# A transformer layer's second feed-forward half step: hidden tiles by way of DRAM, and the output product as seven products of its blocks

## The chip, the cores and the metric

The kernel runs on one core of a Trainium2 chip. The metric is the device time of one execution, in microseconds. A profile is that of a single execution; its durations, and the sums made of them, belong to that execution's own span.

## The reference

One layer of a diffusion backbone over 1024 latent tokens of 1024 features, with 256 context tokens: a SwiGLU half step, token mixers (a short convolution and grouped-query attention side by side), a second SwiGLU half step, and a final RMSNorm. The change lies in the last two, which concern latent tokens alone:

```python
D_MODEL, SEQ, D_FF = 1024, 1024, 2816
def rms_norm(x, g):
    y = x * lax.rsqrt(jnp.mean(x * x, axis=-1, keepdims=True) + EPS)
    return y * g
def modulate(h, shift, scale):
    return h * (1.0 + scale) + shift
def swiglu(h, w_in, w_out):
    a, b = jnp.split(h @ w_in, 2, axis=-1)
    return (jax.nn.silu(a) * b) @ w_out
...
x = x + 0.5 * ml[8] * swiglu(modulate(rms_norm(x, norm3_g[layer]), ml[6], ml[7]),
                              ffn2_w_in[layer], ffn2_w_out[layer])
return rms_norm(x, final_g)
```

`ml[6..8]` are the shift, scale and gate that the layer derives from `c`, one value for each feature. Everything is float32.

## The kernel before, in words

**Layout and precision.** Activations lie with features in partitions: a tile is 128 features by 512 tokens. The 1024 latent tokens are two chunks, C0 and C1. A float32 operand of a product is split into two parts of the matmul's format fp32r, `hi` (a rounded copy) and `lo` (the rest): `split` (l. 186) is a cast on ACT (ScalarE) and a subtraction on DVE (VectorE). A product of two split operands takes three matmuls, hi·hi, hi·lo and lo·hi, all adding into one PSUM bank. "12 matmuls" below is four tiles of the contraction times three.

**Seven products instead of eight.** The class `Winograd` (l. 463) multiplies the weights of two column tiles a and b (blocks: halves of the 1024 input features) with the normalised latents (blocks: halves of the features by C0 and C1). A 2 x 2 block product needs eight products of blocks; Winograd's form needs seven, of sums and differences of the blocks. The seven right operands, from the latents, are made once in `norm0`, `norm1` (l. 499, 525) and stay in SBUF. The left operands are made for each pair of column tiles in `lefts` (l. 572): loads of the raw weights on SP's queue into tiles `raw` (3 buffers), sums `s1`, `s2`, `s3` on POOL (GpSimd), splits into tiles `wl` (4 buffers). `next_first`, `second` and `third` (l. 716 to 740) run the products 1 and 2, then 6, 7, 4, then 5, 3, 12 matmuls each, and add the outcomes from PSUM on DVE in tiles `u`, `v`, `c`, `b`.

**The second half step** is `Winograd.ffn` (l. 742), called at l. 1476 on the object `fast`, over 11 pairs of hidden tiles (2816 hidden features are 22 tiles of 128). For each hidden tile: the seven products of 12 matmuls give a and b of both chunks; `hidden` makes silu(a) * b and splits it into `hid` or `gh`, `gl`, in SBUF. After each pair comes its output product: for both chunks and each of 8 feature tiles, 2 hidden tiles x 3 = 6 matmuls with 512 columns into a fresh bank, 96 matmuls for the pair, and DVE adds the bank, times the gate, to x (one `scalar_tensor_tensor`). The weights for it, four blocks of `w_out`, come through `out_pieces` (l. 451), split into `wo`. With the last pair the second chunk goes in two parts of 256 tokens, and the final norm is run between.

**The final norm.** `final` (l. 1442) is a generator with two steps. The first squares x on ACT, sums the squares on DVE and POOL (`sum_squares`, l. 408), scales x by the gain into `yf` on ACT and derives 1/rms by token with tiny matmuls and a Newton step (`rstd_cols`, l. 240; `rs_a`, `rs_y`). The second turns `yf` back to tokens in partitions, groups of four 128 x 128 transposes into one PSUM bank, copied out times 1/rms by DVE and ACT in turn, and stores. It runs over three pieces: C0, and the two halves of C1. `after2` (l. 1469) says between which additions each step is traced.

**The first half step** already does what the second does not: `spill` (l. 963) stores silu(a) * b of a hidden tile in DRAM (`hd`), and a stage of its own (l. 1018 ff.) loads the hidden tiles back by chunk, splits them, and sums the output product over all 22 tiles in PSUM, without blocks.

**What sets the order.** A scheduler takes the instructions in the order in which they are traced as their priority and places them on each engine by its own estimate of when they can start; each engine then runs its list in that order. The SBUF comes from pools: `atile` (l. 111) takes one of 38 places of 4 KB a partition, `ttile` one of 11 of 2 KB. A tile that asks for a place waits for the last reader of the tile that had it. PSUM has eight banks: five with tag s (`ps_s`, l. 121), two with tag t and one with tag o. All engine calls go through a wrapper, so the profile puts every instruction at line 88; tiles are told apart by name, and names show as their stem (`ps`, `wl`, `raw`).

Of the kernel before, what the change touches and what calls it, by code (L numbers as in the profile page):

```python
# [49 lines left out]
def tile_dit_layer(  # L50
# [29 lines left out]
    class Engine:  # L80
        """An engine whose instructions stay in the order of the trace while strict[0] is set."""
# [72 lines left out]
    # Vectors over features become columns: one row of 128 each, transposed on the chip.  # L154
# [71 lines left out]
    def rsqrt_cols(a, n):  # L226
        """a ** -0.5 for a [P, n] > 0."""
# [12 lines left out]
    def rstd_cols(accs, n, dim):  # L240
        """(sum over accs and partitions + dim * eps) ** -0.5, tokens in partitions: [P, n / P]."""
# [12 lines left out]
    def bcast(y, n):  # L254
        """Columns y over tokens in partitions, as rows in all partitions: PSUM [P, n]."""
# [5 lines left out]
    def later_mod(m, halves=(0, 1), streams=None):  # L261
        """Columns of modulation m for the latents (0) and, where it is used, the context (1), in steps."""
# [54 lines left out]
    def first_mod(m, half, raws):  # L317
        """Half of modulation m of both streams, on the tensor engine alone; in steps: 6 tiles, 2, the columns."""
# [15 lines left out]
    def second_mod(m, half, raws):  # L334
        """The same of the latents alone; in steps: the products of each tile, their parts, their sums, the columns."""
# [23 lines left out]
    def norm_gain(name, m, gname):  # L359
        """g * (1 + scale) * sqrt(D) by stream; the shift is modulation m."""  # L360
# [59 lines left out]
    def modulated_norm(xs, hh, hl, ch, gain, mod, m):  # L420
        """In steps, for other work to be traced between: squares, sums, two halves of the rest."""
# [20 lines left out]
    def run(steps, n=None):  # L442
        """The next n steps (all without n)."""
# [7 lines left out]
    def out_pieces(w, js, spare=False):  # L451
        """Rows of w_out of hidden tiles js, by halves of the columns."""
# [10 lines left out]
    class Winograd:  # L463
        """Products with normalised latents by Winograd's seven products of 2 x 2 blocks.

        Blocks of the weights: two tiles of columns (a, b) by halves of the input features; blocks of
        the activations: halves of the features by halves of the tokens (C0, C1).
        """

        def __init__(self, xs, gain, mod, m, pairs, plain=False, ahead=3, side_from=None):  # L470
            """pairs: columns of each a and b; plain: with all parts of the latents themselves.

            ahead pairs are begun while the second tokens are normalised. side_from: from this pair on
            the plain left operands are given to side(i, operand) too, as 1, 2 (of a), 0, 4 (of b); those of
            the pairs before come after them.
            """
# [3 lines left out]
            self.n_ahead, self.side, self.started, self.n_left = ahead, None, [], 0  # L480
            self.source, self.ready = self.lefts(pairs, side_from), []

        def keep(self, i, k, src, lo_eng=None):
            """Feature tile k of right operand i."""
# [14 lines left out]
        def norm0(self, in_place=False):  # L499
            """In steps: squares, sums, two halves of the rest."""  # L500
# [13 lines left out]
        def square(self, d):  # L514
            """Feature tile d of the second tokens, squared, into the sums."""
            if d == 0:
                self.acc = [ttile("sq_acc")]
            sq = self.acc[0] if d == 0 else ttile("sq")
            act.activation(out=sq, in_=self.xs(d, C1), func=AF.Square)
            if d == KD - 1:  # L520
                self.acc.append(sq)
            elif d:
                dve.tensor_add(out=self.acc[0], in0=self.acc[0], in1=sq)

# [35 lines left out]
        def part_second(self, k):  # L560
            """The parts of tile k of the second tokens, in the place of the values."""
# [5 lines left out]
        def parts(self, k, ch):  # L567
            """Feature tile k of the latents, its two parts."""
# [3 lines left out]
        def lefts(self, pairs, side_from):  # L572
            """Left operands, in the order they are used."""
# [73 lines left out]
        def first(self):  # L647
            """The products with the first tokens alone: what the rest needs, and a of these tokens."""
# [5 lines left out]
        def start(self, norm):  # L654
            """The first products of some pairs, while the second tokens are normalised."""
# [17 lines left out]
        def start_together(self):  # L673
            """The same in steps: P1 of pairs 0, 1; of 2, 3; of each other; then the second products likewise."""
# [854 lines left out]
```

## Time and profile before

| | |
|---|---|
| time, median of 3 runs | 2813.86 us (2812.37 to 2816.64) |
| the profiled execution's span | 2813.7 us |
| granted TensorE clock | 0.9 or more in 37 of the 40 slices of the profile's row PEclk, 0.8 in the others |
| DMA | 298.77 MB, 106 GB/s on the mean |

How to read it: the page gives the busy time of each engine (PE is TensorE's matmuls, PEld its weight loads, SP issues most DMAs) as a share of the span, and the chain of work that ended last, with the share that each engine has in it. The costliest groups of instructions follow, each with its count, mean duration, and the idle time before it. The view by stretches gives the busy time of each engine in a window, with the number of instructions in brackets, then the granted clock, the DMA share and GB/s. A timeline lists instructions in order: the start in us, the busy time, the engine, what it does with the tile's name, its shape, how many of a kind in a row, and in square brackets how long the engine had been idle before and what it had waited for.

### The profile page before, as it was taken

Reading aid. Unit: us, or ns where it says so; the run is one execution under the profiler, and the core shown is the slowest. Engines: PE = TensorE matmul, PEld = TensorE weight load, DVE = VectorE, ACT = ScalarE, POOL = GpSimd, SP = SyncE. Lnnn points to the kernel's source line nnn. Section 1 sums busy time; section 2 is a strip of 40 time slices with the busy share of each in tenths; the row PEclk is TensorE's granted clock in tenths of the full one; section 3 lists DMA queues with packets and bytes.
Section 4 is the critical chain, followed back from the end, with each engine's and each line's share of the span. In section 5 each row is a group of like instructions: output and inputs, shape, how many; then the busy total and the mean of one; then the engine's idle time right before and its main releaser. Section 6 shows DMA issues by size and latency. Waiting matters only on the chain.

```text
span 2813.7 us, 37012 instructions
## 1 busy us (share of the span) xinstructions
PE 2725.5 (97%) x13741; PEld 2286.0 (81%) x13741; DVE 1957.2 (70%) x3218; ACT 1096.5 (39%) x2176; POOL 542.3 (19%) x433
## 2 busy tenths in 40 slices
PE   7898999999999989999999999999998999999998
PEld 4687988888888868888999888887886788888887
DVE  5886688877864387676568377776458766666667
ACT  3524333333433243333345167764245222232225
POOL 2541122121001054323123000000014221212111
PEclk8899999999999989999999999999999999999999
DMA  8264433445974333323313300002532311221111
GB/s 303 97 199 151 145 111 126 130 142 158 309 236 130 104 119 106 105 69 97 105 46 122 111 23 5 12 1 90 170 93 90 111 41 51 60 60 53 46 53 68
DMA packets 346910, 298.77 MB, mean 106 GB/s; under 512 B 25430, under 2 KB 276456, under 8 KB 346728
## 3 DMA queue, kind: packets, MB, share of 16 engines
q1 hardware_dynamic: 346728, 296.40, 32.9%
q8 instruction: 108, 1.77, 0.3%
q14 instruction: 74, 0.61, 0.1%
HBM read 247.54 MB, written 48.76 MB: 105 GB/s over the span
## 4 chain that ended last, share of the span: by engine, by line
PE 83%; DVE 9%; DMA 3%; issue 2%; ACT 2%; SPq 0%; POOL 0%; ACTq 0%; DVEq 0%; POOLq 0%
PE ps L88 73%; PE po L88 6%; PE pt L88 4%; DVE wl L88 2%; DVE r L88 1%; DVE nt L88 1%; DVE macc L88 1%; DMA raw<-in_ffn_w_out_dram 1%; DMA rawm<-in_w_mod_dram 1%; DVE wo L88 1%; DMA hid<-hd 1%; DVE h L88 1%; DVE uc L88 0%; SPq L88 0%; DMA mcol<-mrow 0%
## 5 line engine op out<-in xcount | busy, mean ns | idle before, releaser
L88 PE MATMUL ps<-r,wl 128*128 128x512 f32 x5280 | 1242.0, 394 | 36.9 <-ACT wl L88 12.8
L88 PEld LDWEIGHTS ps<-r,wl 128*128 128x128 f32 x5280 | 995.5, 190 | 256.1 <-ACT wl L88 16.4
L88 ACT CAST wl<-s 128x512 fp32r<-128x512 f32 x256 | 158.6, 620 | 330.3 <-PE ps L88 274.5
L88 ACT CAST wl<-raw 128x512 fp32r<-128x512 f32 x230 | 142.3, 620 | 245.7 <-PE ps L88 165.8
L88 DVE TENSOR_TENSOR wl<-raw,wl 128x512 fp32r<-128x512 f32 x228 | 167.1, 733 | 99.9 <-ACT wl L88 98.8
L88 DVE TENSOR_TENSOR wl<-s,wl 128x512 fp32r<-128x512 f32 x256 | 217.4, 850 | 11.6 <-ACT wl L88 9.8
L88 POOL TENSOR_TENSOR s<-raw,s 128x512 f32<-128x512 f32 x64 | 99.1, 1549 | 624.2 <-DVE wl L88 618.9
L88 PE MATMUL ps<-hid,wh 128*128 128x512 f32 x704 | 217.2, 390 | 1.4 <-ACT wh L88 1.4
L88 ACT CAST wh<-raw 128x1024 fp32r<-128x1024 f32 (+2 forms) x100 | 97.9, 982 | 251.5 <-PE ps L88 208.6
L88 DVE SCALAR_TENSOR_TENSOR x<-ps,gate_l,x 128x512 f32<-128x512 f32 (+1 forms) x200 | 140.7, 726 | 79.1 <-PE ps L88 78.8
L88 POOL TENSOR_TENSOR sq_acc<-sq_acc,sq 128x512 f32<-128x512 f32 (+1 forms) x33 | 41.8, 1268 | 765.4 <-ACT sq L88 764.6
L88 POOL TENSOR_TENSOR s<-raw 128x512 f32<-128x512 f32 x64 | 91.2, 1424 | 399.4 <-DMA raw<-in_ffn_w_in_dram 164.5
L88 DVE TENSOR_TENSOR wl<-raw,wh 128x1024 fp32r<-128x1024 f32 (+1 forms) x92 | 109.6, 1192 | 67.5 <-ACT wh L88 65.8
L88 PEld LDWEIGHTS ps<-hid,wh 128*128 128x128 f32 x704 | 131.7, 188 | 30.2 <-ACT wh L88 2.6
L88 DVE SCALAR_TENSOR_TENSOR macc<-rawm,silu_c,macc 128x512 f32<-128x512 f32 x168 | 141.4, 859 | 12.0 <-DMA rawm<-in_w_mod_dram 11.0
L88 PE MATMUL ps<-hid,wo 128*128 128x512 f32 (+1 forms) x552 | 147.7, 381 | 0.4 <-DVE x L88 0.3
L88 DVE TENSOR_TENSOR u<-u,ps 128x512 f32<-128x512 f32 x168 | 114.3, 680 | 46.6 <-PE ps L88 46.3
L88 PE MATMUL ps<-wh,r 128*128 128x256 f32 x768 | 141.5, 285 | 0.0
L88 PE MATMUL ps<-gh,wo 128*128 128x512 f32 (+1 forms) x368 | 135.5, 380 | 1.5 <-ACT wo L88 1.5
L88 PE MATMUL ps<-hid,wl 128*128 128x512 f32 x352 | 136.5, 389 | 0.0
L88 DVE TENSOR_REDUCE m<-ps 128x1 f32<-128x512 f32 (+1 forms) x192 | 112.7, 595 | 20.9 <-PE ps L88 19.8
L88 DVE TENSOR_TENSOR pts<-pt,pts 128x512 fp32r<-128x512 f32 x160 | 108.7, 683 | 18.8 <-ACT pts L88 18.4
(259 smaller groups left out, 4897.1 us busy)
## 6 DMA issues: line engine op xcount, KB each, us to landing
raw<-in_ffn_w_in_dram SPq DMA_DIRECT2D x114, 512.0 KB, 3.7
raw<-in_ffn_w_out_dram SPq DMA_DIRECT2D x76, 512.0 KB, 4.6
rawm<-in_w_mod_dram SPq DMA_DIRECT2D x128, 256.0 KB, 4.1
raw<-in_w_in_dram SPq DMA_DIRECT2D x57, 512.0 KB, 4.0
hid<-hd SPq DMA_DIRECT2D x44, 256.0 KB, 6.2
rawm<-in_w_mod_dram SPq DMA_DIRECT2D x16, 512.0 KB, 8.1
xd<-x SPq DMA_DIRECT2D x32, 256.0 KB, 8.6
x<-xd SPq DMA_DIRECT2D x32, 256.0 KB, 6.1
```

The source lines that it names most:

```text
L88: inst = getattr(self.engine, name)(*args, **kw)
```

## The change

`Winograd.ffn` is removed. The second half step first makes all 22 hidden tiles with `spill`, that is, silu(a) * b unsplit into DRAM; then `fetch_hidden` loads them back, 22 loads of 512 KB, each with both chunks of one hidden tile, into places of the large pool. Then `row_products` makes the output product as one stage, again by seven products of 2 x 2 blocks: the contraction is 22 hidden tiles in halves of 11 (`nk`), the output 8 feature tiles in halves of four, the tokens C0 and C1. Products are taken in the order 1, 2, 5, 6, 7, 4, 3. Each is 11 steps of 12 matmuls (4 feature tiles x 3) into four PSUM banks that stay for the whole product; an operand is split for each step into `wl` (left, from `ffn2_w_out`) and `wh` (right, from the hidden tiles), four buffers each. The sums for left operands (products 5, 6, 3 in tiles `ws`, 7 in the raw tile) and for right ones (5, 6, 7, 4, in place of the hidden tiles) are all `pool` operations. After each product the four banks go through additions on DVE in tiles `u` (`chain`), and each finished block is added to x by a `scalar_tensor_tensor` of 512 columns (`add3`): 24 of them, and 8 of 256 columns in product 3.

Product 3 (the first four features of C1) runs in two halves of 256 tokens; its 22 operands are split once into tiles of the large pool (`kept`) and used by both halves. `final` now begins with features 4 to 7, has an extra step between these and the rest, makes its scaled copies `yf` on DVE instead of ACT, and gives the squares of the last four features to the tiny matmuls one by one, without POOL. `after3` places it: the first two steps of C0 after product 4, its transposes after step 4 of the first half of product 3, the others further behind. `square` counts its calls in place of asking for feature 0. Comments and docstrings are dropped.

```diff
-        def ffn(self, w_o, gate, last_chunks, after):
...
+    def row_products(w, nk, raws, add, after=lambda i, k: None, halves=False):
...
+        def rows(t, k, lower, left, n=1):
+            o, c = k * P + R * lower, 512 * (not left)
+            load(t, w[o : o + n * P, c : c + 512].rearrange("(a p) n -> p a n", p=P))
...
+        def lefts(i):
+            for k in range(nk):
+                if i in (1, 2, 4, 3, 6):
+                    if k % 2 == 0:
+                        t, n = raw_tile(), min(2, nk - k)
+                        rows(t[:, :n], k, i in (2, 4, 3), i != 4, n)
+                    src = t[:, k % 2]
+                if i == 5:
+                    t = raw_tile()
+                    rows(t[:, :1], k, False, False)
+                    rows(t[:, 1:], k, True, False)
+                    if k % 2 == 0:
+                        sums[k] = atile("ws", (P, 2, 512))
+                    s = sums[k - k % 2][:, k % 2]
+                    pool.tensor_add(out=s, in0=t[:, 0], in1=t[:, 1])
+                    src = s
+                elif i in (6, 3):
+                    s = sums[k - k % 2][:, k % 2]
+                    if i == 6:
+                        pool.tensor_sub(out=s, in0=s, in1=src)
+                    else:
+                        pool.tensor_sub(out=s, in0=src, in1=s)
+                    src = s
+                elif i == 7:
+                    t = raw_tile()
+                    load(t[:], w[k * P : (k + 1) * P, :].rearrange("p (a n) -> p a n", a=2))
+                    pool.tensor_sub(out=t[:, 0], in0=t[:, 0], in1=t[:, 1])
+                    src = t[:, 0]
+                yield src
+        def right(i, k):
+            (b11, b12), (b21, b22) = ((t[:, 0], t[:, 1]) for t in (raws[k], raws[nk + k]))
+            if i == 5:
+                pool.tensor_sub(out=b11, in0=b12, in1=b11)
+            elif i == 6:
+                pool.tensor_sub(out=b11, in0=b22, in1=b11)
+            elif i == 7:
+                pool.tensor_sub(out=b12, in0=b22, in1=b12)
+            elif i == 4:
+                pool.tensor_sub(out=b11, in0=b11, in1=b21)
+            return {2: b21, 7: b12, 3: b22}.get(i, b11)
...
+        for i in (1, 2, 5, 6, 7, 4, 3):
+            if i == 3 and halves:
+                kept = []
+                for h in range(2):
+                    a, ps = h * 256, [ps_s(256) for _ in range(4)]
+                    for k, left in enumerate(lefts(i) if h == 0 else kept):
+                        if h == 0:
+                            kept.append((parts(left, None), parts(right(i, k), None)))
+                        l, r = kept[k]
+                        step(ps, k, l, r[:, :, a : a + 256])
+                        after(8 + h, k)
+                    for d in range(4):
+                        add(d, ("l", 512 + a, 256), ps[d])
+                    after(8 + h, nk)
+                break
+            ps = [ps_s() for _ in range(4)]
+            for k, left in enumerate(lefts(i)):
+                step(ps, k, parts(left, "wl"), parts(right(i, k), "wh"))
+                after(i, k)
+            for d in range(4):
+                if i == 1:
+                    chain[d] = ttile("u")
+                    act.copy(out=chain[d], in_=ps[d])
+                elif i == 2:
+                    c = ttile("c")
+                    dve.tensor_add(out=c, in0=chain[d], in1=ps[d])
+                    add(d, C0, c)
+                elif i == 5:
+                    add(d, C1, ps[d])
+                    add(d + 4, C1, ps[d])
+                elif i == 6:
+                    dve.tensor_add(out=chain[d], in0=chain[d], in1=ps[d])
+                    add(d, C1, chain[d])
+                elif i == 7:
+                    dve.tensor_add(out=chain[d], in0=chain[d], in1=ps[d])
+                    add(d + 4, C1, chain[d])
+                elif i == 4:
+                    dve.tensor_sub(out=chain[d], in0=chain[d], in1=ps[d])
+                    add(d + 4, C0, chain[d])
...
     def final(ch):
         s, o, n = ch
-        acc = sum_squares(xs, ch)
-        yk = []
-        for k in range(KD):
-            y = atile("yf")
-            act.activation(out=y[:, :n], in_=xs(k, ch), func=AF.Copy, scale=gf[:, k : k + 1])
-            yk.append(y)
-        rstd = rstd_cols([acc], n, D)
+        order = (4, 5, 6, 7, 0, 1, 2, 3)
+        acc, sqs, yk = ttile("sq_acc", n), [], {}
+        for k in order:
+            if k == 0:
+                yield
+            sq = ttile("sq", n) if k != 4 else acc
+            act.activation(out=sq, in_=xs(k, ch), func=AF.Square)
+            if k in (5, 6, 7):
+                dve.tensor_add(out=acc, in0=acc, in1=sq)
+            elif k < 4:
+                sqs.append(sq)
+            if k % 2 == 0:
+                y2 = atile("yf", (P, 2, 512))
+            yk[k] = y2[:, k % 2, :n]
+            dve.tensor_scalar(out=yk[k], in0=xs(k, ch), scalar1=gf[:, k : k + 1], scalar2=None, op0=ALU.mult)
+        rstd = rstd_cols([acc] + sqs, n, D)
         yield
...
+    fast.start(fast.norm1())
+    for j in range(NH):
+        u, c = fast.next_first()
+        v, b = fast.second(u)
+        spill(c, b, j, C0)
+        spill(*fast.third(u, v), j, C1)
+    hs = fetch_hidden()
...
+    def after3(i, k):
+        if (i, k) == (4, NH // 2):
+            run(finals[0], 2)
+        elif (i, k) == (8, 4):
+            run(finals[0])
+        elif (i, k) == (8, 7):
+            run(finals[1], 1)
+        elif (i, k) == (8, NH // 2):
+            run(finals[1], 1)
+            run(finals[2], 1)
+        elif (i, k) == (9, 5):
+            run(finals[1])
+    row_products(ffn2_w_out[0], NH // 2, hs, add3, after3, halves=True)
     run(finals[2])
```

More of the change, by code (lines that the diff above doesn't have):

```diff
@@ new lines, in row_products, with raw_tile, parts, step @@
+    def row_products(w, nk, raws, add, after=lambda i, k: None, halves=False):
+        R = P * nk
+        def rows(t, k, lower, left, n=1):
+            o, c = k * P + R * lower, 512 * (not left)
+            load(t, w[o : o + n * P, c : c + 512].rearrange("(a p) n -> p a n", p=P))
+        def raw_tile():
+            return wpool.tile([P, 2, 512], F32, tag="raw", name=uniq("raw"), bufs=3)
+        sums = {}
+        def lefts(i):
[38 more added lines that the diff above has]
+            return {2: b21, 7: b12, 3: b22}.get(i, b11)
+        def parts(src, tag):
+            if tag:
+                t = wpool.tile([P, 2, 512], F32R, tag=tag, name=uniq(tag), bufs=W_BUFS)
+            else:
+                t = atile("kept", (P, 2, 512), F32R)
+            split(src, t[:, 0], t[:, 1])
+            return t
+        def step(ps, k, l, r):
+            for d in range(4):
+                wh, wl = (l[:, v, d * P : (d + 1) * P] for v in range(2))
+                matmul(ps[d], wh, r[:, 0], start=k == 0, stop=False)
+                matmul(ps[d], wh, r[:, 1], start=False, stop=False)
+                matmul(ps[d], wl, r[:, 0], start=False, stop=k == nk - 1)
+        chain = {}
+        for i in (1, 2, 5, 6, 7, 4, 3):
[17 more added lines that the diff above has]
+                after(i, k)
+            for d in range(4):
+                if i == 1:
[17 more added lines that the diff above has]
+                    add(d + 4, C0, chain[d])
+                else:
+                    add(d, C1, ps[d])
+            after(i, nk)
```

67 lines of the change are left out of this document (16 added, 51 removed).

## The prediction

> **What bounds the kernel now.** First the page: its busy shares and the head of the chain that ended last.
>
> ```profile
> span 2813.7 us, 37012 instructions
> PE 2725.5 (97%) x13741; PEld 2286.0 (81%) x13741; DVE 1957.2 (70%) x3218; ACT 1096.5 (39%) x2176; POOL 542.3 (19%) x433
> PE 83%; DVE 9%; DMA 3%; issue 2%; ACT 2%; SPq 0%; POOL 0%; ACTq 0%; DVEq 0%; POOLq 0%
> ```
>
> TensorE is the bound. The median of the three runs is 2813.86 us, so next to nothing lies around the profiled span of 2813.7, and I add up against the span. Second, the busy times by stretch, for the half step that changes (columns: length, PE, PEld, DVE, ACT, POOL, granted clock, DMA share, GB/s).
>
> ```profile
> 2300.00:2760.00 460.00, 460.00 (x2031) 380.85 (x2030) 301.26 (x432) 127.51 (x216) 80.46 (x60) 1.00 0.17 51
> 2790.00:2813.70 23.70, 15.37 (x115) 13.99 (x114) 15.21 (x53) 14.33 (x32) 2.57 (x4) 0.87 0.44 179
> ```
>
> From 2300 to 2760 us PE never rests, while VectorE works 65% and GpSimd 17% of the time: there a matmul saved is time saved, as long as nothing else fills up. Third, the timelines: ACT's copies of u, one per hidden tile, and PE at the last output product.
>
> ```profile
> 2317.71 0.59 ACT L88 COPY u<-ps 128x512 f32<-128x512 f32 x1 [19.46 <-PE ps L88]
> 2377.55 0.59 ACT L88 COPY u<-ps 128x512 f32<-128x512 f32 x1 [20.95 <-PE ps L88]
> 2771.75 1.30 PE L88 MATMUL ps<-hid,wo 128*128 128x512 f32 x5
> 2799.11 0.28 PE L88 MATMUL ps<-gl,wo 128*128 128x256 f32 x1
> 2799.24 0.28 PE L88 MATMUL ps<-gh,wo 128*128 128x256 f32 x1
> ```
>
> Two hidden tiles with their output products take 59.84 us: 2 x 7 x 12 + 96 = 264 matmuls, so 0.2267 us for 512 columns. 256 columns start some 0.12 us apart. The last Winograd product ends at 2771.75.
>
> **1. PE work.** Removed: ten pairs x 96 x 0.2267 = 217.6 us, all of it before 2771.75, and the last pair (48 of 512 columns, 96 of 256), 22.4. Added: six products of 11 row tiles x 4 features x 3 = 132 matmuls each, 179.5 us, and the seventh in two halves, 264 x 0.12 = 31.7. Net 28.8 us less. The 192 additions to x out of PSUM go too, but DVE had room for them: nothing.
>
> The front of the half step keeps its order up to the first pair. The one wait of PE for an output weight there (1.5 us at 2199.8) goes; the denser pairs behind it may cost as much, since in the mixers' stage, equally dense, PE lost 2 us after its norm. I count zero (bounds -2 and +3), so the new stage begins at 2771.75 - 217.6 = 2554.1.
>
> **2. The hidden tiles come back from DRAM.** 22 loads of 512 KB. Two find free places early; the other 20 wait for the Winograd operands of the last hidden tile, the first of which come free 16 us before the stage begins, as they stand ahead of further weights in SP's queue. The nearest thing is the first half step, which reloads its hidden tiles in the same way:
>
> ```profile
> 740.00:750.00 10.00, 10.00 (x46) 8.03 (x45) 8.89 (x12) 8.20 (x13) 0.00 (x0) 1.00 1.05 389
> 770.72 0.73 PE L88 MATMUL ps<-hid,wh 128*128 128x512 f32 x2 [0.64 <-ACT wh L88]
> 772.22 0.73 PE L88 MATMUL ps<-hid,wh 128*128 128x512 f32 x2 [0.77 <-ACT wh L88]
> ```
>
> It moved up to 389 GB/s and cost PE 1.4 us. Here 11.5 MB, with the weights and the spills between, need about 31 us at 370 GB/s; they end 15 us into the stage, and the weights queued behind them are wanted at 16. I take 1.4 (bounds 0 and 6).
>
> **3. GpSimd and VectorE in products 5, 6, 7.** The change puts 88 sums of 128x512 on GpSimd: 11 left and 11 right operands each for products 5, 6 and 7, 11 rights for 4, 11 lefts for 3. Its order on the engine lets 20 to 24 of these run in products 1 and 2; 50 fall between the end of product 2 and that of 7. What one costs beside VectorE is seen where the norm fills both engines:
>
> ```profile
> 2154.76 1.72 POOL L88 TENSOR_TENSOR nt<-h,h 128x512 f32<-128x512 f32 x1
> 2156.43 1.73 POOL L88 TENSOR_TENSOR r<-nt,r 128x512 fp32r<-128x512 f32 x1
> 2158.13 1.72 POOL L88 TENSOR_TENSOR s<-raw,s 128x512 f32<-128x512 f32 x1
> 2175.08 1.29 POOL L88 TENSOR_TENSOR s<-s,raw 128x512 f32<-128x512 f32 x1
> 2176.33 1.73 POOL L88 TENSOR_TENSOR s<-raw,raw 128x512 f32<-128x512 f32 x1
> 2153.59 0.67 DVE L88 TENSOR_TENSOR uc<-uc,ps 128x512 f32<-128x512 f32 x1
> 2156.95 1.77 DVE L88 TENSOR_TENSOR r<-h,r 128x512 fp32r<-128x512 f32 x1
> 2158.64 1.76 DVE L88 TENSOR_TENSOR r<-nt,r 128x512 fp32r<-128x512 f32 x1
> 2162.01 0.68 DVE L88 TENSOR_TENSOR nt<-h,nt 128x512 f32<-128x512 f32 x1
> 2162.61 0.68 DVE L88 TENSOR_TENSOR r<-nt,r 128x512 fp32r<-128x512 f32 x1
> 2205.40 4.70 DVE L88 SCALAR_TENSOR_TENSOR x<-ps,gate_l,x 128x512 f32<-128x512 f32 x7 [3.06 <-PE ps L88]
> ```
>
> Alone, GpSimd starts a sum every 1.25 us and VectorE a subtraction every 0.60. Together each takes 1.69 for one of both: a GpSimd sum holds VectorE up by 1.09, unless that reads PSUM (the 0.67 row). Each step of a product (12 matmuls, 2.72 us of PE) needs two subtractions of two SBUF tiles, left and right. Over products 5 to 7 VectorE has 66 of them, 39.6 us; 8 additions to x from SBUF, 5.3; 16 operations out of PSUM, 10.1; and 42 sums that hold it up (8 of the 50 fit beside PSUM reads), 45.8: 100.8 us, where PE needs 3 x 29.9 = 89.7. **Loss 11 us.** Bounds: 0, if the four buffers of each operand take it up, and 22, if boundaries and the three raw buffers add as much again; 11 is the plain sum. In products 1, 2 and 4 the same sum stays below PE (50 of 55 us, 26 of 29.9).
>
> **4. The last product and the final norm.** Here the fixed order is against PE. In before, several banks turn the outputs, and the tail looks so:
>
> ```profile
> 1314.54 0.88 DVE L88 TENSOR_SCALAR y<-u,cols 128x512 f32<-128x512 f32 x2
> 2792.87 2.35 PE L88 MATMUL ps<-ident,yf 128*128 128x128 f32 x20
> 2794.66 1.27 ACT L88 ACTIVATE ot<-ps,rs_y 128x512 f32<-128x512 f32 x2 [0.43 <-DVE rs_y L88]
> 2799.56 0.48 DVE L88 SCALAR_TENSOR_TENSOR x<-ps,gate_l,x 128x256 f32<-128x256 f32 x1 [0.17 <-PE ps L88]
> 2800.45 1.02 ACT L88 ACTIVATE sq<-x 128x256 f32<-128x256 f32 x3
> 2803.52 0.60 PE L88 MATMUL pt<-ones,sq_acc 128*128 128x1 f32 x4
> 2804.16 0.16 DVE L88 TENSOR_SCALAR rs_a<-pt 128x2 f32<-128x2 f32 x1 [0.70 <-PE pt L88]
> 2806.12 0.16 DVE L88 SCALAR_TENSOR_TENSOR rs_y<-rs_t,rs_y 128x2 f32<-128x2 f32 x1
> 2807.30 1.26 ACT L88 ACTIVATE ot<-ps,rs_y 128x512 f32<-128x512 f32 x2 [1.50 <-PE ps L88]
> ```
>
> After the sixth product (call its end 0) VectorE first does 4 additions (the last ends at 2.0), 3 more of x and of squares (1.9), 8 scalings of 0.40 (3.2), and then the first pair of splits of product 3: PE waits until about 9. Until the scale of the first 512 tokens is known come 9 splits of 0.6, 2 sums of squares and 3 half ones, and the 2.2 us from rs_a to the last rs_y: 19.5. The four accumulators of a half leave one of the pool's five banks, and eight groups of transposes, ahead of the sixth step on PE, pass through it one by one: 0.65 to copy out, 0.5 to turn (4 of 0.118), some 0.3 for the two handovers, 1.45 x 7 + 0.65 = 11, so 30.5. Then 12 splits and 4 scalings, 8.4, and the last step: **the first half ends at 39**, where its matmuls alone are 15.8. The second half has its operands: 15.8, 16 transposes 1.9, small sums and the wait for the banks 2: 19.7. The tail, from the last matmul, was 2813.7 - 2799.24 = 14.5; GpSimd's and VectorE's sums of squares behind the last square (2.9) go, and ACT no longer copies out 0.8 later than VectorE: 10.8. Bounds for this part together: 59 (the first half at 28, its matmuls, its turns and the first wait) and 89 (rival B).
>
> **Sum.** 2554.1 + 179.5 + 1.4 + 11.2 + 39 + 19.7 + 10.8 = 2815.7 us: the 28.8 us are given back, **+0.1%**. Forecast 2816.
>
> **The clock.** After an idle stretch PE is slow:
>
> ```profile
> 2153.82 1.22 PE L88 MATMUL ps<-r,wl 128*128 128x512 f32 x2 [5.99 <-ACT wl L88]
> 2157.08 5.06 PE L88 MATMUL ps<-r,wl 128*128 128x512 f32 x11 [2.04 <-DVE wl L88]
> 2163.34 6.12 PE L88 MATMUL ps<-r,wl 128*128 128x512 f32 x25 [1.20 <-DVE r L88]
> ```
>
> Behind 6 us of rest, 11 matmuls took 0.46 us each; some 6 us of work later it is 0.245. My 39 has this once, under the splits that it waits for anyway. The Trainium skill, "TensorE: Matmul & The Clock Gate", section "HAM oscillation — how this bites in real kernels", speaks against the change here: rest longer than about 3.4 us puts the array back to half rate, and a kernel that does so again and again runs cold throughout. By it the sum would be that of rival B; the rows show one such fall, not a row of them.
>
> **Rivals.**
> A, faster, 2795 us: the stage stays bound by PE. The sums of products 5 to 7 disappear behind the operands made ahead (-11.2), and in the last product the splits do not queue behind the turned outputs, so that the first half ends at 30. For it: VectorE's 65% and GpSimd's 17% today, 460 of 460 us on PE. Against: the lockstep rows.
> B, slower, 2835 us: PE rests twice in the last product, for some 9 and 11 us, and so goes to half rate and stays there, since its work comes in short groups. Place: both halves of product 3; price: 132 matmuls of the second half at 0.24, +15.8, and about 4 us of the first behind the transposes. It decides from the point where dense work does not follow a rest for about 6 us. For it: the rows above and the 0.87 after 2790. Against: the second half is dense.
>
> **How the numbers follow.** Forecast (the gain given back, 2803 to 2827) 0.50; A (2788 to 2803) 0.30; B (2827 to 2845) 0.20. 0.2%, about what a measurement of this kernel tells from no change, is 5.6 us, so the lines are at 2808.2 and 2819.5. The forecast's own spread lies 0.10 below, 0.25 between and 0.15 above them. With A and B: faster 0.40, same 0.25, slower 0.35. The range leaves a tenth out at each end: 2793 to 2836.
>
> **What would show it.** Step 1: 792 output matmuls of 512 columns and 264 of 256 where there were 1008 and 96, the wider ones 0.227 apart. Step 2: PE's wait on hid or raw around the stage's beginning, 0 to 6 us. Step 3: VectorE over 90% busy in products 5 to 7, its splits at 1.7 us beside GpSimd's 1.7, PE waiting for them at 3.3 us a step; if PE is gapless there, step 3 is wrong and A holds. Step 4: after product 4 about 9 us of rest, eight groups of transposes 1.45 us apart, and some 70 us from there to the end; if it is near 55, step 4 is wrong. B: a granted clock near 0.6 in the last 40 us.

## The result, and the profile after

The changed kernel took **2833.43 us** (median of four runs, 2829.05 to 2838.28) where the kernel before took 2813.84 (four runs): a ratio of 1.0065, with an interval of 1.0051 to 1.0079. It is slower by 19.6 us between the medians; the forecast was 2816, no change, in a range of 2793 to 2836.

The same lines of the page as were read before, now of the changed kernel:

```profile
span 2830.2 us, 37466 instructions
PE 2715.7 (96%) x13757; PEld 2279.2 (81%) x13757; DVE 1976.0 (70%) x3169; ACT 1124.3 (40%) x2222; POOL 676.7 (24%) x512
...
PE 80%; DVE 10%; DMA 4%; issue 2%; ACT 2%; POOL 1%; SPq 1%; DVEq 0%; ACTq 0%; POOLq 0%
```

TensorE is busy for 10 us less and yet the end comes later; its share of the last chain falls from 83% to 80%. This execution took 2832.19 us, so 2.0 us lie around the span. The prediction took that as nothing, since it held the median of several runs against the span of one execution; but in the kernel before 1.8 us lie there too (an execution of 2815.47 us has a span of 2813.7).

The busy times by stretch of the new stage (columns as before: length, PE, PEld, DVE, ACT, POOL, granted clock, DMA share, GB/s). The borders are the first output matmul, two places in products 2 and 6, the end of product 4, and the span's end:

```profile
2552.19:2612.00 59.81, 57.91 (x253) 46.92 (x252) 41.55 (x43) 25.98 (x46) 34.85 (x23) 1.00 0.60 213
2612.00:2665.00 53.00, 43.94 (x166) 33.16 (x165) 53.00 (x38) 14.63 (x26) 52.94 (x33) 0.90 0.44 141
2665.00:2750.63 85.63, 85.63 (x377) 70.35 (x376) 68.01 (x83) 32.62 (x58) 39.61 (x27) 1.00 0.35 117
2750.63:2830.20 79.57, 57.63 (x409) 54.04 (x408) 45.15 (x110) 26.71 (x54) 5.13 (x4) 0.80 0.13 54
```

The loss sits in two of the four. In the second stretch VectorE and GpSimd are busy without a break, and VectorE gets only 38 operations through in 53 us, 1.39 us each. In the last one TensorE rests for 22 us of 80. In the third, on the other hand, TensorE has no rest at all.

TensorE's timeline shows where the rests are. The number in front of the arrow is the rest before a group, behind it is what ended it:

```profile
2569.90 2.11 PE L88 MATMUL ps<-wh,wl 128*128 128x512 f32 x8 [1.23 <-ACT wl L88]
2572.61 51.29 PE L88 MATMUL ps<-wh,wl 128*128 128x512 f32 x223 [0.60 <-DVE wl L88]
2625.10 3.28 PE L88 MATMUL ps<-wh,wl 128*128 128x512 f32 x13 [1.20 <-DVE wh L88]
2631.83 13.35 PE L88 MATMUL ps<-wh,wl 128*128 128x512 f32 x45 [3.45 <-DVE wh L88]
2645.38 3.02 PE L88 MATMUL ps<-wh,wl 128*128 128x512 f32 x12 [0.20 <-DVE wh L88]
2648.77 3.01 PE L88 MATMUL ps<-wh,wl 128*128 128x512 f32 x12 [0.38 <-DVE wh L88]
2652.17 3.01 PE L88 MATMUL ps<-wh,wl 128*128 128x512 f32 x12 [0.39 <-DVE wh L88]
2655.58 0.96 PE L88 MATMUL ps<-wh,wl 128*128 128x512 f32 x3 [0.39 <-DVE wh L88]
2658.93 3.94 PE L88 MATMUL ps<-wh,wl 128*128 128x512 f32 x10 [2.40 <-DVE wh L88]
2663.55 87.09 PE L88 MATMUL ps<-wh,wl 128*128 128x512 f32 x382 [0.67 <-DVE wh L88]
2758.06 1.22 PE L88 MATMUL ps<-kept,kept 128*128 128x256 f32 x4 [7.42 <-ACT kept L88]
...
2762.21 7.45 PE L88 MATMUL ps<-kept,kept 128*128 128x256 f32 x40 [1.72 <-DVE kept L88]
2769.49 0.28 PE L88 MATMUL pt<-ones,sq_acc 128*128 128x1 f32 x2
...
2777.12 1.00 PE L88 MATMUL ps<-ident,yf 128*128 128x128 f32 x4
2778.95 0.66 PE L88 MATMUL ps<-ident,yf 128*128 128x128 f32 x4 [0.83 <-ACT ot L88]
...
2787.76 1.12 PE L88 MATMUL ps<-ident,yf 128*128 128x128 f32 x4 [0.84 <-DVE ot L88]
...
2790.01 9.09 PE L88 MATMUL ps<-kept,kept 128*128 128x256 f32 x68 [0.28 <-DVE kept L88]
...
2817.47 0.96 PE L88 MATMUL ps<-kept,kept 128*128 128x256 f32 x6
```

From this the terms of the sum can be measured one by one. Product 4 ends at 2663.55 + 87.09 = 2750.6, the first half of product 3 at 2790.01 + 9.09 = 2799.1, the second at 2818.4.

| step | forecast | measured |
|---|---|---|
| the stage begins | 2554.1 | 2552.2 |
| 792 matmuls of six products at 0.2267 | 179.5 | 179.5 |
| wait for a load (1.23) | 1.4 | 1.2 |
| the rest of what six products lose (198.4 in all) | 11.2 | 17.7 |
| product 3, first half | 39 | 48.5 |
| product 3, second half | 19.7 | 19.3 |
| tail | 10.8 | 11.8 |
| end of the span | 2815.7 | 2830.2 |

### The profile page after: what moved, and what is told of

It is laid out like the page before. It is cut to its first block, busy times and chain, and to the rows that moved or that the text cites. A ratio compares the mean times of both kernels' runs of the same rounds, so it can differ in the third digit from the quotient of the medians.

```text
span 2830.2 us, 37466 instructions
## 1 busy us (share of the span) xinstructions
PE 2715.7 (96%) x13757; PEld 2279.2 (81%) x13757; DVE 1976.0 (70%) x3169; ACT 1124.3 (40%) x2222; POOL 676.7 (24%) x512
## 4 chain that ended last, share of the span: by engine, by line
PE 80%; DVE 10%; DMA 4%; issue 2%; ACT 2%; POOL 1%; SPq 1%; DVEq 0%; ACTq 0%; POOLq 0%
PE ps L88 70%; PE po L88 6%; PE pt L88 4%; DVE wl L88 2%; DMA raw<-in_ffn_w_out_dram 1%; DVE macc L88 1%; DVE r L88 1%; DVE nt L88 1%; DVE wh L88 1%; DMA rawm<-in_w_mod_dram 1%; SPq L88 1%; DMA hid<-hd 1%; DVE h L88 1%; DVE x L88 1%; DVE uc L88 0%
## 5 line engine op out<-in xcount | busy, mean ns | idle before, releaser
L88 ACT CAST wl<-raw 128x512 fp32r<-128x512 f32 x274 | 169.5, 620 | 336.4 <-PE ps L88 238.0
L88 DVE TENSOR_TENSOR wl<-raw,wl 128x512 fp32r<-128x512 f32 x272 | 208.1, 766 | 120.3 <-ACT wl L88 118.6
L88 DVE TENSOR_TENSOR wl<-s,wl 128x512 fp32r<-128x512 f32 x256 | 221.7, 867 | 12.4 <-ACT wl L88 10.6
L88 POOL TENSOR_TENSOR sq_acc<-sq_acc,sq 128x512 f32<-128x512 f32 (+1 forms) x24 | 33.0, 1375 | 724.0 <-ACT sq L88 723.3
L88 PE MATMUL ps<-wh,wl 128*128 128x512 f32 x792 | 187.5, 397 | 11.0 <-DVE wh L88 9.1
L88 PEld LDWEIGHTS ps<-wh,wl 128*128 128x128 f32 x792 | 150.6, 192 | 47.7 <-DVE wh L88 13.2
L88 DVE TENSOR_TENSOR u<-u,ps 128x512 f32<-128x512 f32 x180 | 122.4, 681 | 54.4 <-PE ps L88 51.6
L88 DVE SCALAR_TENSOR_TENSOR macc<-rawm,silu_c,macc 128x512 f32<-128x512 f32 x168 | 141.9, 862 | 11.8 <-DMA rawm<-in_w_mod_dram 10.7
L88 PEld LDWEIGHTS ps<-wh,r 128*128 128x128 f32 x768 | 120.5, 192 | 0.0
```

What stands on the lines that cost most here:

```text
L88: inst = getattr(self.engine, name)(*args, **kw)
```

## The experiments

**How they are compared.** Up to the first output matmul all kernels hold the same program, yet in the traces the stage begins anywhere from 2550.5 to 2560.7. So I compare two lengths from each trace: **six products**, from the first output matmul to the end of product 4 (198.4 us in the changed kernel), and **the rest**, from there to the end of the span (79.6). Each is a length in one execution. Five kernels that have the six products alike (the change, e3, e4, e8, e11) agree on them within 0.4 us; e10, whose last product is that of the change, has 78.9 for the rest, so 0.7 us there is no difference. The medians and ratios to the kernel before stand beside them.

| kernel | six products | the rest | median | ratio to before |
|---|---|---|---|---|
| the change | 198.4 | 79.6 | 2833.4 | 1.0065 (1.0051 to 1.0079) |
| e1 sums left out | 181.2 | 78.2 | 2811.0 | 0.9990 (0.9978 to 1.0001) |
| e2 sums on VectorE | 187.4 | 81.0 | 2825.8 | 1.0039 (1.0026 to 1.0052) |
| e10 right sums on VectorE | 197.4 | 78.9 | 2833.6 | 1.0071 (1.0058 to 1.0084) |
| e3 transposes in two banks | 198.4 | 74.3 | 2831.1 | 1.0058 (1.0043 to 1.0073) |
| e4 filled rest | 198.0 | 83.0 | 2835.9 | 1.0083 (1.0065 to 1.0101) |
| e5 early splits | 198.4 | 79.0 | 2830.8 | 1.0059 (1.0044 to 1.0074) |
| e8 transposes later | 198.2 | 71.4 | 2820.5 | 1.0029 (1.0017 to 1.0040) |
| e11 squares added up | 198.3 | 79.7 | 2832.5 | 1.0066 (1.0049 to 1.0082) |
| e9 = e2 + e3 + e5 + e8 | 189.0 | 65.6 | 2805.6 | 0.9974 (0.9962 to 0.9985) |
| e12 = e9 + e11 | 188.4 | 58.7 | 2802.2 | 0.9954 (0.9942 to 0.9967) |
| e13 = e12, five steps early | 188.3 | 55.3 | 2800.0 | 0.9950 (0.9936 to 0.9963) |

### e1: the sums left out

In `row_products` the `pool` operations go; each product takes a plain block.

```diff
-                    pool.tensor_add(out=s, in0=t[:, 0], in1=t[:, 1])
-                    src = s
+                    src = t[:, 0]
...
             if i == 5:
-                pool.tensor_sub(out=b11, in0=b12, in1=b11)
+                pass
...
```

> Leaves out the 88 sums of operands on GpSimd: every product takes plain blocks, so the result is not the layer's. Loads, splits, matmuls and additions stay as they are. In the changed kernel the first six products took 198.2 us (2552.2 to 2750.4), their matmuls alone 179.5. Theory (GpSimd's sums hold VectorE up, and the rests that this makes slow TensorE's clock): the six products take 181 to 184 us, no rest over 1 us in products 5 to 7, granted clock 1.00 there, the whole about 2818. Rival (VectorE's own splits and additions, or the loads of the weights, set the pace): 195 us or more, the whole 2829 or more.

Six products in 181.2 us, as the theory had it (the whole, at 2811.0, came out 7 us below what it gave). Of them 1.23 are a wait near the start; behind it 720 matmuls follow without a rest:

```profile
2568.44 163.49 PE L88 MATMUL ps<-wh,wl 128*128 128x512 f32 x720 [1.23 <-ACT wl L88]
```

So everything that the six products lose beyond loads comes with the sums. VectorE's own splits and additions, and the loads, are not it.

### e2: the sums on VectorE

```diff
...
-                pool.tensor_sub(out=b11, in0=b12, in1=b11)
+                dve.tensor_sub(out=b11, in0=b12, in1=b11)
...
```

and so for each of the sums.

> The 88 sums are done by VectorE in place of GpSimd; nothing else. Theory (the two engines hold each other up; VectorE alone has the time): a sum costs VectorE 0.60 us, 53 us in all, beside some 115 that it has in these 180 us; splits keep at 0.60, the six products take 181 to 188 us, the whole 2818 to 2824. Rival (VectorE has no room in products 5 to 7, whoever does the sums): the six products take 198 us or more, the whole 2833 or more.

187.4 us: VectorE does 88 operations more and the six products are 11 us shorter, as the theory had it (the whole, at 2825.8, is 2 us above its range). Why is seen in the groups of VectorE's instructions (count, busy time, mean ns), for the same split, first in the changed kernel from 60 to 158 us behind the beginning of the stage, then in the like stretch of e2:

```profile
L88 DVE TENSOR_TENSOR wh<-hid,wh 128x512 fp32r<-128x512 f32 x30 | 45.5, 1518 | 0.0
```

```profile
L88 DVE TENSOR_TENSOR wh<-hid,wh 128x512 fp32r<-128x512 f32 x34 | 23.3, 689 | 0.0
```

The split is the same instruction; beside GpSimd it takes 1518 ns on the mean, alone 689. What e2 still loses (6.7 us beyond the load wait) lies mainly in the same place as before: the 53 us from 59.8 us behind the stage's beginning.

```profile
2619.40:2672.40 53.00, 49.56 (x208) 39.63 (x207) 52.96 (x88) 19.24 (x35) 0.00 (x0) 0.97 0.41 129
```

VectorE is full there still, with 88 operations in place of 38.

### e10: half of them

```diff
         def right(i, k):
-                pool.tensor_sub(...)
+                dve.tensor_sub(...)
```

> Only the 44 sums of right operands go to VectorE, those of left ones stay on GpSimd. Theory (each GpSimd sum costs VectorE about a microsecond where it stands beside a split): about half of the loss stays, the six products take 190 to 194 us, where all sums on GpSimd took 198.2 and all on VectorE 187.4. Rival (the loss has a threshold): 188 or less, or 197 or more.

197.4: almost nothing is won, and the theory as I had put it, half the sums for half the loss, fell; the rival's number (197 or more) came. The row of the same stretch shows why:

```profile
2615.70:2668.70 53.00, 43.80 (x164) 33.79 (x163) 52.83 (x54) 13.75 (x25) 33.74 (x21) 0.87 0.40 131
```

GpSimd has 21 sums in the stretch where it had 33: at 1.09 us each VectorE is held up by 13 us less. But 13 of VectorE's 54 operations in it are the moved sums themselves, and they too are slow beside the left sums that stay on GpSimd:

```profile
L88 DVE TENSOR_TENSOR hid<-hid,hid 128x512 f32<-128x512 f32 x13 | 16.1, 1245 | 0.2
```

They take more than what was freed. VectorE gets 25 splits done in the stretch, as many as in the changed kernel, and TensorE's work in it stays where it was (43.80 us busy after 43.94). So the price of a sum fits, and what counts is whether VectorE has time in this stretch: it got that only when GpSimd was silent (e2).

### e3: two banks for the transposes

```diff
-                pt = ps_s()
+                pt = ps_t()
```

> The final norm's transposes go into the two PSUM banks of tag t in place of the one that is free of tag s. Theory (the eight groups in the first half of product 3 pass one bank one by one, 1.5 to 1.95 us each, 2777.1 to 2788.5): they take some 0.8 us each, 6 to 7 us together, and the whole gets 4 to 6 us shorter, about 2828. Rival (the splits of the last six steps, which stand behind the copies on ScalarE and VectorE, set the end of the half): the groups get closer, the whole stays within 2 us of 2833.

The rest falls to 74.3 us, 5.3 less. TensorE's timeline: eight transposes at a time, the first and the last of four such groups,

```profile
2783.24 1.09 PE L88 MATMUL pt<-ident,yf 128*128 128x128 f32 x8
...
2788.18 1.09 PE L88 MATMUL pt<-ident,yf 128*128 128x128 f32 x8 [0.41 <-DVE ot L88]
```

where there were groups of four with 0.84 us of rest ahead of each. All eight groups take 6.0 us here, where the last seven took 11.8. The median of 2831.1 shows less of it: it is 2.3 us below that of the change, where the theory gave 4 to 6, and so it lies as near to 2833 as the rival had it (within 2 us). The runs differ by more than that ahead of the stage (this trace's stage begins 5.3 us later than that of the change), so the gain is read from the length in the trace; the whole does not show it.

### e4: the rest after product 4 filled

Thirty more matmuls, into a spare bank.

```diff
...
+                if i == 4 and k == nk - 1:
+                    po = ps_o()
+                    for f in range(30):
+                        matmul(po, fl[:, 0, :P], fr[:, 0], start=f == 0, stop=f == 29)
```

> Thirty more matmuls of 512 columns into a spare bank, whose outcome nothing reads, are put behind product 4: some 6.8 us in the 7.4 us in which TensorE rests there. Theory (the rest is what slows TensorE behind it): the 40 matmuls of 256 columns behind it take 4.8 to 5.2 us in place of 7.45, the 16 behind the small sums 2.0 in place of 3.27, the granted clock from 2750 to 2770 rises from 0.66 to 0.9 or more, and the whole gets 3 to 5 us shorter. Rival (the clock is not what paces this part, the splits of VectorE and ScalarE are): the matmuls run faster, but the first half ends no earlier, the whole stays within 1 us of 2833 or gets longer.

The rest is 83.0 us: not shorter. (The traced execution is the slowest of four, with a stage that begins 8.5 us later than that of the change.) The first two 20 us behind product 4 in e4,

```profile
2758.60:2778.60 20.00, 16.87 (x97) 14.57 (x95) 18.35 (x30) 10.92 (x22) 6.11 (x4) 0.91 0.01 5
2778.60:2798.60 20.00, 13.84 (x65) 11.17 (x65) 4.95 (x16) 4.18 (x8) 0.00 (x0) 0.54 0.20 79
```

and in the changed kernel:

```profile
2750.63:2770.63 20.00, 10.86 (x60) 10.02 (x60) 18.04 (x30) 10.91 (x22) 5.13 (x4) 0.66 0.00 0
2770.63:2790.63 20.00, 14.74 (x82) 12.23 (x82) 7.73 (x23) 6.95 (x13) 0.00 (x0) 0.68 0.20 79
```

The granted clock of the first 20 us did rise, to 0.91 (48 matmuls of 256 columns took 7.26 us where 40 had taken 7.45), and VectorE did the same 30 operations in them. So in these 20 us the clock is not what paces the half. In the next 20, among the small matmuls and the transposes, it falls lower than in the change (0.54 after 0.68); what the full clock there would bring, e4 does not show.

### e5: splits ahead of the additions

```diff
...
+                if i == 4 and k >= 7 and len(kept) < 3:
+                    kept.append((parts(next(last), None), parts(right(3, len(kept)), None)))
```

> The operands of the first three steps of product 3 are split during the last steps of product 4, ahead of its additions; nothing else. In the changed kernel the time from the end of product 4 to the end of the span is 79.6 us, with a rest of 7.4 us first and the transposes' second group 26.5 us behind product 4. Theory (the rest is the wait for ScalarE's first copies, which stand behind squares of x, and it is lost for good): a rest of 3 us or less, and the 79.6 fall to 74 to 76. Rival (the chain from product 4's additions over squares and small sums to the transposes sets the half, whatever TensorE does meanwhile): the rest goes, but the transposes begin 25 us or more behind product 4 as before, and the 79.6 stay above 78.

The rest of 7.4 us behind product 4 is gone, the matmuls there run at full clock (36 in 4.47 us), and nothing is won (79.0):

```profile
2750.56 4.47 PE L88 MATMUL ps<-kept,kept 128*128 128x256 f32 x36
...
2774.85 1.08 PE L88 MATMUL ps<-ident,yf 128*128 128x128 f32 x4 [3.10 <-DVE ot L88]
```

TensorE now rests ahead of the transposes instead. They begin 24.1 us behind product 4, a little earlier than the rival had it (25), and after 26.5 in the changed kernel; the last group ends at 2787.5, 36.8 behind product 4 after 38.2. The rival holds in the whole.

### e8: the transposes in the second half

```diff
-        elif (i, k) == (8, 4):
-            run(finals[0])
...
+        elif (i, k) == (9, 1):
+            run(finals[0])
```

> The transposes of the first 512 tokens are traced after step 1 of the second half of product 3, not after step 4 of the first; nothing else. Theory (in the first half they hold up the splits, which stand behind their copies on ScalarE and VectorE, and TensorE's own order): the first half ends 35 to 39 us behind product 4 in place of 48.5, the second grows by the 4 us of 32 transposes, and the 79.6 us fall to 71 to 74. Rival (they cost the same wherever they stand, since one bank is free in either half): 78 or more.

The rest falls to 71.4 us, 8.2 less, as the theory had it. In the first half 93 matmuls now follow each other behind the small sums,

```profile
2771.57 14.01 PE L88 MATMUL ps<-kept,kept 128*128 128x256 f32 x93
```

and 87 of them are the first half's last, which therefore ends some 36 us behind product 4 (which ends at 2748.7 here) in place of 48.5. In the second half groups of four transposes stand between 27 matmuls each and cost no rest. This is the largest single piece of the last product.

### e11: the squares added up

```diff
-            if k in (5, 6, 7):
+            if k in (5, 6, 7) or n == 512 and k < 4:
```

> The squares of all eight features of the first 512 tokens are added up by VectorE (four more additions of 0.6 us), so that TensorE gets 8 small matmuls with the ones in place of 40, which take 4.4 us in its queue ahead of the transposes; nothing else. Theory (TensorE's own queue sets the moment at which the scale is known): the scale is known 3 to 4 us earlier than the 25.6 us behind product 4, and the 79.6 us fall to 75.5 to 77. Rival (VectorE's queue sets it, and the additions only move the time there): 79 or more.

79.7: the theory that the small matmuls in TensorE's queue set the scale's time fell.

```profile
2769.86 1.02 PE L88 MATMUL pt<-ones,sq_acc 128*128 128x1 f32 x8 [0.71 <-DVE sq_acc L88]
2773.99 0.93 PE L88 MATMUL ps<-ident,yf 128*128 128x128 f32 x4 [3.11 <-DVE ot L88]
```

Eight small matmuls in place of 40, but they wait for VectorE's additions, and the transposes wait for the scale. Those begin 24.9 us behind product 4 (2749.1) in place of 26.5.

### e9, e12, e13: together

e9 takes e2, e3, e5 and e8 together, e12 adds e11's edit, e13 splits five steps early (`k >= 6 and len(kept) < 5`).

> All four together: sums on VectorE, transposes in the banks of tag t and in the second half, the first three steps of product 3 split early. Theory (two causes, the sums beside VectorE and the transposes in the first half): six products in 181 to 188 us, 62 to 67 us from the end of product 4 to the end, the whole 2802 to 2808, faster than the kernel before. Rival (the edits of the last product take away the same wait, or VectorE, now with the sums, is late with the early splits): 72 us or more behind product 4, the whole 2812 or more.

> The kernel with the four edits (sums on VectorE, transposes in the banks of tag t and in the second half, three steps split early; 65.5 us behind product 4, median 2805.6) with the squares of the first 512 tokens added up by VectorE. Theory (small matmuls stand in TensorE's queue for 6.4 us at the slowed clock in the first half): 60 to 63 us behind product 4, the whole 2800 to 2803. Rival (VectorE's queue paces the first half by now): 65 or more, the whole 2805 or more.

> The same with the operands of five steps of product 3 split during product 4 in place of three. Theory (the rest of 3.3 us behind the early steps is the wait for the next split, behind the additions and scalings of x): the rest goes or halves, the first half has no slowed stretch, 58 to 61 us behind product 4, the whole 2797 to 2801. Rival (it is product 4 that becomes late, since VectorE has the splits besides): six products 191 us or more, the whole no shorter than with three.

All three went as the theory had it, but for six products of e9, 189.0 (six matmuls of product 3 stand in that length already), and for the rest of e12 and e13, 58.7 and 55.3 us, 1.3 and 2.7 better than the ranges. What won nothing alone wins here: in the traces e11's edit takes 6.9 us off e9, where it took nothing off the change, and two more early steps 3.3. The medians show only 3.3 and 2.2 us of that (the runs of e9 lie between 2800 and 2811), and the intervals of their ratios overlap. In e13 the first half of product 3 is dense:

```profile
2742.50 9.03 PE L88 MATMUL ps<-kept,kept 128*128 128x256 f32 x74
2752.10 16.06 PE L88 MATMUL ps<-kept,kept 128*128 128x256 f32 x130 [0.57 <-DVE kept L88]
```

So seven products of blocks in a stage of their own can win: with these edits e13 is 0.5% faster than the kernel before (0.37 to 0.64%), about 14 us of the 28.8 that TensorE saves. The edits to the final norm were not tried in the kernel before, so it is not shown that the whole gain belongs to the seven products. Of what is missing, 8.8 us lie in six products still (188.3, with six matmuls of product 3 in it, less 179.5).

## Why the prediction was right or wrong

**The whole.** The direction, that the 28.8 us saved are given back on VectorE and in the last product, was right; the size was not, since some 20 us more are lost. Of 14.5 us missing in the sum, 9.5 are the first half of product 3, 6.5 the sums beside VectorE, 1.0 the tail, and the earlier start takes 1.9 off. A further 2.0 us lie around the span. 2833 lies outside the forecast's own spread (2803 to 2827), in the bracket that was given to rival B (2827 to 2845, chance 0.20). B's mechanism did not come, so it is luck that the range of 2793 to 2836, whose upper end stood there for B, holds the result.

**Step 1, PE work: right.** 792 and 264 matmuls, the start 1.9 us off, the second half at 19.3 us within 0.4.

**Step 2, the reload: right.** 1.2 us after 1.4.

**Step 3, GpSimd and VectorE: right in mechanism, too small.** (100.8 less 89.7 is 11.1; the sum has 11.2.) The splits went to 1.7 us where GpSimd worked, as the rows of before had shown at the norm, and e2 shows that it is GpSimd's being at work that makes them slow. (The Trainium skill, "GPSIMD Engine Reference", section "1. Specifications", has the two engines share their SBUF interfaces, with contention where a VectorE instruction has two inputs there; 1518 ns beside 689 agrees.) Two things made it 17.7 and not 11.2. First, I took VectorE's 100.8 us against TensorE's 89.7 over all three products. The deficit lies in 53 us of it, from the additions behind product 2 into product 6, where GpSimd has 33 sums; in the rest of product 6 and in 7 VectorE has time left, which comes too late. The rests that VectorE causes add up to 9.7 us; 0.6 of them lie in product 1 already, where the splits run beside GpSimd's early sums (e1, without sums, does not have this rest). Second, TensorE runs slowly behind the rests. The stretch around the longest, in small slices, and one slice behind the rest of 2.40 us:

```profile
2628.00:2632.00 4.00, 0.55 (x3) 0.17 (x2) 4.00 (x4) 0.68 (x2) 4.00 (x3) 0.89 0.60 204
2632.00:2635.00 3.00, 3.00 (x8) 2.32 (x9) 3.00 (x2) 0.00 (x0) 3.00 (x3) 0.50 0.39 134
2635.00:2638.00 3.00, 3.00 (x9) 2.33 (x8) 3.00 (x3) 1.14 (x2) 3.00 (x3) 0.51 0.28 109
2638.00:2641.00 3.00, 3.00 (x15) 2.47 (x14) 3.00 (x3) 1.14 (x2) 3.00 (x2) 1.00 0.54 169
...
2658.00:2661.00 3.00, 2.07 (x5) 1.49 (x6) 3.00 (x4) 0.00 (x0) 3.00 (x3) 0.57 0.52 147
```

Behind the rest of 3.45 us the clock is at half for some 6 us of work. The 45 matmuls there take 13.35 us where 10.2 are their time at 0.2267, and the 10 behind the rest of 2.40 take 3.94 where it is 2.3: 4.8 us. The other 3.2 of the 8.0 (17.7 less 9.7) are the ends of the groups, each of which takes 0.2 to 0.7 us more than its count times 0.2267 (12 matmuls 3.02 for 2.72). The prediction counted a slow clock for product 3 alone. That the slow clock follows the rests is argued from the order of the rows: e1 takes both away together, and e2, which keeps one rest of 2.38 us, keeps a slow stretch behind it:

```profile
2636.00:2639.00 3.00, 2.78 (x7) 2.16 (x8) 3.00 (x6) 0.00 (x0) 0.00 (x0) 0.61 0.75 231
```

**Step 4, the last product: right in place, the first half too small by 9.5.** The forecast had the rest of 9 us (7.4), the single bank (e3: 5.3 us of the loss) and the transposes that hold up the half (e8: 8.2). What failed is the 19.5 us "until the scale is known": the transposes' second group began 26.5 us behind product 4, where the sum has 20.5 (19.5, the first copy of 0.65 and a handover). VectorE's own work ahead of the scale was sized well: its last sum of squares ends 18.1 us behind product 4, where the sum has 17.3. But then VectorE waits for TensorE:

```profile
2774.05 0.16 DVE L88 TENSOR_SCALAR rs_a<-pt 128x4 f32<-128x4 f32 x1 [5.35 <-PE pt L88]
```

These 5.35 us are the wait for the 40 small matmuls with the ones. They take 4.4 us in TensorE's queue and stand behind 40 matmuls at a partly slowed clock (7.45 us where 4.8 is their time at 0.12). My sum, of VectorE's work alone, had no term for them. But no single one of them is the cause: e4 and e5 took away the rest, e11 the small matmuls, and e11's wait at this place falls to 1.2 us only behind four more additions on VectorE. e5 and e11 brought the second group forward by 2.4 and 1.6 us, the last group's end by 1.5 and 0.7, and of that 0.6 and nothing reached the end of the span. The rows show where it went: all groups of transposes that follow take 1.1 us there, and the matmuls behind them some 0.9 us more (70 in 10.26 us in e5, 72 in 10.44 in e11, 68 in 9.09 in the change). The groups came some 1.5 us apart at first, as forecast with 1.45, then 1.95, with transposes that take 1.1 us in place of 0.66 at a clock near half; I had taken them at the full one. Behind them the sum has 8.4 us of scalings and splits on VectorE, which took 8.4, and nothing for the last step; but TensorE still had 72 matmuls to do, and they took 10.6. So of the 9.5 us, 6.0 lie ahead of the second group, 1.4 in the groups and 2.1 behind them.

**The rivals.** A did not come. B named the last product, both halves of it, but its mechanism was wrong: its 15.8 us were to come from a half clock in the second half, and that ran at 0.12 us a matmul; the last 40 us have a granted clock of 0.93, where B had 0.6. A slow clock is there in the first 40 us (0.66 and 0.68), and e4 shows that raising it in the first 20 of them alone buys nothing. How much the slow clock among the transposes costs by itself, no run here shows. The Trainium skill's "TensorE: Matmul & The Clock Gate", section "HAM oscillation — how this bites in real kernels", was weighed as speaking for B: it has rests longer than about 3.4 us end in half rate. The trace agrees for the rest of 3.45 us, but half rate came behind the one of 2.40 us too. That the kernel runs cold throughout is not seen here, since in the six products dense work had the full rate back within some 7 us, and the whole execution has a clock of 0.978.

**"What would show it"** served: PE's wait for splits was to be 3.3 us a step (twelve matmuls and 0.38 of rest, 3.40, in the slow stretch), and some 70 us from product 4 to the end would have been step 4 right: it was 79.6.

## What to carry to other kernels

Before work is given to an idle GpSimd, look at what VectorE does at that moment: here a sum on GpSimd cost 1.1 us of VectorE's time, unless VectorE was reading PSUM, and doing the sum on VectorE itself cost 0.6. Reckon an engine's load over the stretch between two boundaries in which the work must be done, not as a mean over a stage. And where several queues meet ahead of one wait, taking a delay out of one shows nothing until the next one is gone too: of edits that alone won 0.6, 5.3, 8.2 and 0 us of the rest, the four together, with two more early steps and the sums on VectorE, won 24.

## What the runs showed of the hardware

The half clock came in pieces: some 6 us of work behind the rest of 3.45, and after a rest of only 2.40 us (the row at 2658.93) 10 matmuls took 3.94 us where 2.3 would do, though shorter rests of 0.4 us ahead of it had cost nothing of the kind. Among the transposes of e5, in groups of four with rests of 0.8 us, the granted clock stayed at 0.50 from 2774.85 to 2787.1. VectorE's gated additions to x are slowed by GpSimd as well where their other operand lies in SBUF (1640 ns in the changed kernel, 746 in e2, four of each), and not where it lies in PSUM (735 and 746, eight of each).
